# Smaller adaLN weight slabs, the vector part's loads one step ahead, and 512-column runs for the gate's matvec

## The chip, the core and the metric

The kernel runs on one core of one Trainium2 chip. A core has a tensor engine (PE, whose weight loads the profile lists apart as PEld), a vector engine (DVE), a scalar engine (ACT), GpSimd (POOL), the sync engine (SP) that mostly issues DMAs, and 16 DMA engines behind the queues. Each engine works through its own instructions in their order and waits on semaphores for the others. The metric is the device time of one execution in microseconds; less is better.

## The reference

One layer of a flow-matching backbone, for 128 context tokens and 256 latent tokens, D = 2048 channels, all in fp32. What matters here is the modulation that comes from the condition vectors c and c_ctx through the matrix ada_w (2048 x 12288), and where its six parts are used:

```python
def _adaln(cond, ada_w, ada_b):
    mod = jax.nn.silu(cond) @ ada_w + ada_b
    return mod.reshape(cond.shape[0], N_MOD, D_MODEL)
...
shift_a, scale_a, gate_a, shift_f, scale_f, gate_f = [mod[:, i][:, None, :] for i in range(N_MOD)]
h = _rmsnorm(x, norm_w[0]) * (1 + scale_a) + shift_a
proj = h @ w_in
...
q, k, v, o, g, u = jnp.split(proj, [M, 2 * M, 3 * M, 4 * M, 4 * M + N_GATES * N_HEADS], axis=-1)
...
hm, C, n, m = _mlstm_bidir(q, k, v, gates, C0.astype(f32), n0.astype(f32), m0.astype(f32))
...
hp = _pool_mixer(u, pool_w, pool_scale, grid_w)
mix = jnp.concatenate([hm, hp], axis=-1) @ w_out
x = x + gate_a * _rmsnorm(mix, norm_w[1])
h = _rmsnorm(x, norm_w[2]) * (1 + scale_f) + shift_f
y = jnp.square(jax.nn.relu(h @ w1)) @ w2
x = x + gate_f * _rmsnorm(y, norm_w[3])
```

The mLSTM has 8 heads of 128 channels and runs over three chunks of 128 tokens (the context one and two latent ones) in both directions. Each of the six parts i = 0 to 5 of the modulation is a product of two vectors (c_ctx and c) with 2048 columns of ada_w: 16 MB are read for it once.

## The kernel before

**Products.** Every fp32 weight tile of 512 KB is loaded into one of three raw buffers (`load_w`, L114 to L132), split by ACT into a high part (L126) and by DVE into a low part (L127), four buffers of each, and multiplied in three matmuls, L135 to L137 (high by high, low by high, high by low). A tile of q, k or o is 24 such matmuls of 384 columns. The program goes through u and v of the input projection (s = 0 to 7, two channel tiles each), then q and k for four pairs of heads, then o, the output projection wo, and the MLP.

**The modulation.** Shift_a and scale_a (i = 0, 1) are made by the tensor engine ahead of and beside u and v (`first_ada`), 256 columns at a time. `ada_mat` (L203) takes up to four parts of up to 256 columns. A part is 16 rows of ada_w per partition; per 512 KB slab (four rows of 256 columns) it has four matmuls, each with 32 rows of output in its own quarter of the array (rows 32 g to 32 g + 31 of one PSUM bank, g = j mod 4). When all parts have been added up, ACT copies the sum to SBUF (L223), small matmuls on it (L226) turn it into columns, and DVE adds the bias (`ada_finish`, L234). For gate_a (i = 2), `mid_mat` calls it twice with four parts of 256 columns: 34 steps, 32 of them a slab and a group of four matmuls. Scale_f and shift_f (i = 4, 3) are made by DVE: `ada_vec` (L244 to L274) does 512 columns in eight steps, each a load of 512 KB (two rows of 512 columns, L250) and four DVE instructions that multiply and add (L255, L257) into `ada_acc`; then four matmuls add up the partitions (L265), ACT copies (L267), and two small matmuls (L270) make columns: 10 steps for each of eight calls. Gate_f (i = 5) is made in the MLP, by one ada_mat run and three ada_vec runs.

**What sets the order.** `Feed` (L142) gives a side job a number of steps per call, and each product calls its feeds after every weight tile: gate_a 0.75 steps, the vector part 80/76 steps, one step of the attention of the pair of heads before, and so on. In the attention of a pair (names `..._0` to `..._3`), `num` and `cu` are products with v, `C1` is the state that DVE carries to the next chunk (L579), `hs` is the output that DVE normalises (L598, L601), and `hT` (L640) are its transposes on PE. The tile scheduler then lays the instructions of PE, DVE and ACT into one fixed order each. All weight and slab loads go through SP's one queue in one order, where a load waits until its buffer is free, and everything behind it on SP waits too. A load on SP also waits until the eighth load before it has landed.

**Buffers.** The ada slabs share four buffers of 4 KB per partition (tag `ada`, `N_ADA = 4`); in their places the last rows of the gate, `gf` (L923), lie at the end of the MLP. The copies of L223 and L267 share two small tiles (tag `adasb`).

## Time and profile before

| | |
|---|---|
| median of three runs | 1767.98 us (1766.83 to 1768.8) |
| span of the profiled execution | 1766.4 us |
| its instructions | 24738 |
| loads of ada_w | 192 of 512 KB |
| DMA traffic | 326.15 MB, 185 GB/s over the span |

Times in the profile count from the start of the span. A row of the timeline has the start of an instruction or of a run of alike ones, its duration, engine, line, operation, `output<-inputs`, shape and count; brackets at its end tell how long the engine sat idle before it and who released it. A row of the waits has engine and line, what it waited for, the sum in us, the number of times and the longest. A row of the windows has, for each engine, busy time and number of instructions in a stretch of time, then the granted PE clock as a share of full speed, the busy share of the DMA engines and GB/s.

### The profile page before, as it was taken

To read this page: it belongs to the slowest core of one execution; us is meant where nothing else is said; L and a number is where in the kernel's file an instruction comes from. 1 tells how busy PE (TensorE), PEld (TensorE's weight loads), DVE (VectorE), ACT (ScalarE), POOL (GpSimd) and SP (SyncE) were. 2 spreads that over 40 slices of the span, in tenths; PEclk is the share of its full clock that TensorE was granted. 3 is DMA by queue.
4 is the path that set the end of the run, shared out by engine and by line. 5 is a ranking of instruction groups with operands and counts; after the bars stand their busy time and mean duration, and the time that the engine had idled before them with its cause. 6 is when DMAs were issued, how large, how long until landed. Compare 5 with 4: busy or idle time off the path is not lost.

```text
span 1766.4 us, 24738 instructions
## 1 busy us (share of the span) xinstructions
PE 1719.2 (97%) x9643; PEld 1539.2 (87%) x9643; DVE 1067.4 (60%) x1756; ACT 627.3 (36%) x1047; POOL 129.7 (7%) x172
## 2 busy tenths in 40 slices
PE   6999999998999999999999999999999999999997
PEld 3777898887999989988988988988988998998986
DVE  3667877787898849763546644475444443443446
ACT  4322343443434336532432432332332332332332
POOL 0000021222101133110000000000000000000100
PEclk9999999999999999999999999999999999999999
DMA  9888988887777774574345544454434354344543
GB/s 304 279 263 286 299 261 231 253 251 213 232 238 235 237 250 156 185 225 131 120 130 162 175 130 121 130 167 122 129 120 131 120 168 131 120 130 136 165 141 107
DMA packets 250436, 326.15 MB, mean 185 GB/s; under 512 B 14096, under 2 KB 185808, under 8 KB 249936
## 3 DMA queue, kind: packets, MB, share of 16 engines
q1 hardware_dynamic: 242096, 303.74, 54.1%
q0 software_dynamic: 6560, 18.97, 4.3%
q10 hardware_dynamic: 1664, 1.87, 0.3%
q8 instruction: 75, 1.23, 0.3%
q14 instruction: 41, 0.34, 0.1%
HBM read 313.98 MB, written 10.55 MB: 184 GB/s over the span
## 4 chain that ended last, share of the span: by engine, by line
PE 86%; DMA 5%; issue 3%; DVE 2%; POOL 2%; ACT 1%; SPq 0%; ACTq 0%; DVEq 0%; POOLq 0%
PE y L855 10%; PE y L856 10%; PE y L857 10%; PE acc_w L135 9%; PE acc_w L137 9%; PE acc_w L136 9%; DMA ada_raw<-in_ada_w_dram 3%; PE acc_wo L135 3%; PE acc_wo L136 2%; PE acc_wo L137 2%; PE ada L218 2%; PE acc_o L135 1%; PE acc_o L137 1%; PE acc_o L136 1%; PE u L379 1%
## 5 line engine op out<-in xcount | busy, mean ns | idle before, releaser
L127 DVE TENSOR_TENSOR lo_w<-raw_w,hi_w 128x1024 fp32r<-128x1024 f32 x256 | 313.9, 1226 | 440.7 <-ACT hi_w L126 440.3
L126 ACT ACTIVATE hi_w<-raw_w 128x1024 fp32r<-128x1024 f32 x256 | 271.3, 1060 | 666.2 <-PE acc_w L136 302.1
L135 PE MATMUL acc_w<-h2h,hi_w 128*128 128x386 f32 x1024 | 347.8, 341 | 2.4 <-ACT h2h L805 2.4
L137 PE MATMUL acc_w<-h2h,lo_w 128*128 128x386 f32 x1024 | 347.5, 339 | 0.0
L136 PE MATMUL acc_w<-h2l,hi_w 128*128 128x386 f32 x1024 | 347.2, 339 | 0.0
L257 DVE SCALAR_TENSOR_TENSOR ada_acc<-ada_raw,sg,ada_acc 128x512 f32<-128x512 f32 x330 | 237.5, 767 | 21.8 <-DMA ada_raw<-in_ada_w_dram 21.7
L135 PEld LDWEIGHTS acc_w<-h2h,hi_w 128*128 128x128 f32 x1024 | 193.9, 190 | 5.2 <-ACT h2h L805 3.0
L136 PEld LDWEIGHTS acc_w<-h2l,hi_w 128*128 128x128 f32 x1024 | 193.8, 189 | 0.9 <-issue 0.4
L137 PEld LDWEIGHTS acc_w<-h2h,lo_w 128*128 128x128 f32 x1024 | 193.5, 189 | 0.0
L218 PE MATMUL ada<-ada_raw,cT 128*32 128x256 f32 x832 | 61.5, 397 | 5.1 <-DMA ada_raw<-in_ada_w_dram 5.0
L879 DVE TENSOR_TENSOR y<-y,y 128x512 f32<-128x512 f32 x81 | 55.7, 691 | 11.8 <-PE y L857 11.3
L126 ACT ACTIVATE hi_wo<-raw_wo 128x1024 fp32r<-128x1024 f32 x32 | 34.1, 1067 | 67.1 <-PE acc_wo L136 27.9
L846 ACT ACTIVATE z<-z,bz 128x128 f32<-128x128 f32 (+1 forms) x128 | 47.9, 442 | 11.3 <-DVE z L844 11.2
L127 DVE TENSOR_TENSOR lo_wo<-raw_wo,hi_wo 128x1024 fp32r<-128x1024 f32 x32 | 38.7, 1218 | 19.3 <-ACT hi_wo L126 19.3
L379 PE MATMUL v<-hi_v,hh 128*128 128x384 f32 (+1 forms) x144 | 49.0, 341 | 0.0
L381 PE MATMUL v<-hi_v,hl 128*128 128x384 f32 (+1 forms) x144 | 47.2, 328 | 0.0
L380 PE MATMUL v<-lo_v,hh 128*128 128x384 f32 (+1 forms) x144 | 46.9, 326 | 0.0
L774 POOL DMA_DIRECT2D gf_dram<-gfT x1 | 0.5, 519 | 626.8 <-DVE bz L843 626.8
L135 PE MATMUL acc_k<-hh,hi_k 128*128 128x384 f32 x128 | 45.4, 355 | 0.0
L218 PEld LDWEIGHTS ada<-ada_raw,cT 128*32 128x32 f32 x832 | 19.8, 110 | 28.9 <-issue 14.5
L135 PE MATMUL acc_o<-hh,hi_o 128*128 128x384 f32 x128 | 44.7, 349 | 0.0
L135 PE MATMUL acc_q<-hh,hi_q 128*128 128x384 f32 x128 | 44.4, 347 | 0.0
(940 smaller groups left out, 3621.1 us busy)
## 6 DMA issues: line engine op xcount, KB each, us to landing
raw_w<-in_w_dram SPq DMA_DIRECT2D x256, 512.0 KB, 3.7
ada_raw<-in_ada_w_dram SPq DMA_DIRECT2D x192, 512.0 KB, 5.1
raw_wo<-in_w_out_dram SPq DMA_DIRECT2D x32, 512.0 KB, 4.9
raw_u<-in_w_in_dram SPq DMA_DIRECT2D x16, 512.0 KB, 7.4
raw_q<-in_w_in_dram SPq DMA_DIRECT2D x16, 512.0 KB, 5.8
raw_k<-in_w_in_dram SPq DMA_DIRECT2D x16, 512.0 KB, 5.2
raw_o<-in_w_in_dram SPq DMA_DIRECT2D x16, 512.0 KB, 5.3
raw_v<-in_w_in_dram SPq DMA_DIRECT2D x16, 384.0 KB, 7.8
```

Source lines behind the costliest of these rows:

```text
L126: nc.scalar.activation(hi[:, 0:n], raw[:, 0:n], AF.Copy)
L127: low = lambda: nc.vector.tensor_tensor(lo[:, 0:n], raw[:, 0:n], hi[:, 0:n].bitcast(F32), op=ALU.subtract)
L135: nc.tensor.matmul(ps, lh, rh, start=start, stop=False)
L136: nc.tensor.matmul(ps, lh, rl, start=False, stop=False)
L137: mm3.ins = nc.tensor.matmul(ps, ll, rh, start=False, stop=stop).ins
L218: nc.tensor.matmul(ps[32 * g:32 * g + 32, 0:w], cT[:, j, 6 - 2 * b:38 - 2 * b], raw[:, a, :], start=b == 0 and j < 4, stop=b == n - 1 and ...
L257: nc.vector.scalar_tensor_tensor(acc[:, g, :], raw[:, a, :], cj, acc[:, g, :], op0=ALU.mult, op1=ALU.add)
L379: nc.tensor.matmul(acc[i][:, 0:n], xh[:, sl], hi[:, k, :], start=k == 0, stop=False)
L855: nc.tensor.matmul(acc, xh[:, s], hi, start=k == 8 * ch, stop=False)
L856: nc.tensor.matmul(acc, xh[:, s], lo, start=False, stop=False)
L857: nc.tensor.matmul(acc, xl[:, s], hi, start=False, stop=k == 8 * ch + 7)
L879: nc.vector.tensor_tensor(dst, acc[i], dst, op=ALU.add)
```

## The change

- **Slabs.** The ada buffers are eight of 2 KB per partition in place of four of 4 KB: the same 16 KB. A load is 256 KB in place of 512 KB everywhere, so there are twice as many (one part of the very first step, which uses another tag, is left as it was).
- **The gate's run.** `mid_mat` calls ada_mat once with four parts of 512 columns: 17 steps. A step has four loads of 256 KB, one for each of its four matmuls of 512 columns, and there are 16 groups of four in place of 32 groups of four with 256 columns. The sum fills a whole PSUM bank, so the small matmuls behind it go to a second bank. The rate is 17/46 of a step per call.
- **The vector part.** `ada_vec` issues the two loads of a step one step ahead of the DVE work on them, in an 11th step per call. The rate goes from 80/76 to 88/76, so that it takes as many calls as before.
- **Around it.** The copies share one tile of 512 columns in place of two of 256. The tail's gate rows are eight tiles of 512 columns in place of four of 1024. Comments and docstrings are taken out; line numbers shift by up to 15.

```diff
-N_ADA = 4
+N_ADA = 8
...
+    def ada_tile(tag, nj, w, name):
+        return wp.tile([P, nj, w], F32, tag=tag, name=name, bufs=N_W if tag == "lo" else N_ADA)
...
     def ada_mat(parts, tags=("ada",)):
         n, nk = len(parts), parts[0][2]
-        w, nj = nk * P, 8 // nk
+        w = nk * P
         ps = bank(f"ada_{parts[0][0]}_{parts[0][1]}")
         for b, (i, k0, _) in enumerate(parts):
             c0 = i * D + k0 * P
+            tag = tags[b % len(tags)]
+            nj = (8 if tag == "lo" else 4) // nk
             for j0 in range(0, 16, nj):
-                tag = tags[b % len(tags)]
-                raw = wp.tile([P, nj, w], F32, tag=tag, name=f"ada_raw_{i}_{k0}_{j0}", bufs=N_W if tag == "lo" else N_ADA)
+                raw = ada_tile(tag, nj, w, f"ada_raw_{i}_{k0}_{j0}")
                 nc.sync.dma_start(raw, aw[:, j0:j0 + nj, c0:c0 + w])
...
-                if b < n - 1 or j0 + nj < 16:
+                if (j0 + nj) % 4 == 0 and (b < n - 1 or j0 + nj < 16):
                     yield
-        sb = wp.tile([P, 256], F32, tag="adasb", name=f"ada_sb_{parts[0][0]}_{parts[0][1]}", bufs=2)
+        sb = wp.tile([P, 512], F32, tag="adasb", name=f"ada_sb_{parts[0][0]}_{parts[0][1]}", bufs=1)
         nc.scalar.activation(sb[:, 0:w], ps[:, 0:w], AF.Copy)
         yield
+        if w > 256:
+            ps = bank(f"adaf_{parts[0][0]}_{parts[0][1]}")
+        o = 0 if w > 256 else 256
...
     def ada_vec(i, q):
...
+        def load(t):
+            raws = [ada_tile("ada", 1, 512, f"ada_raw_{i}_{q}_{j}")[:, 0, :] for j in (2 * t, 2 * t + 1)]
+            for a, raw in enumerate(raws):
+                nc.sync.dma_start(raw, aw[:, 2 * t + a, c0:c0 + 512])
+            return raws
+
+        raws = load(0)
+        yield
         for t in range(8):
-            raw = wp.tile([P, 2, 512], F32, tag="ada", name=f"ada_raw_{i}_{q}_{t}", bufs=N_ADA)
-            nc.sync.dma_start(raw, aw[:, 2 * t:2 * t + 2, c0:c0 + 512])
+            ahead = load(t + 1) if t < 7 else None
...
+            raws = ahead
...
     def mid_mat():
-        for i, hb in MID[:6 - N_VEC]:
-            yield from ada_mat([(i, 8 * hb + 2 * b, 2) for b in range(4)])
+        yield from ada_mat([(2, 4 * b, 4) for b in range(4)])
...
-    ada1 = Feed(mid_mat(), max(0.75, 17 * (6 - N_VEC) / 76))
-    ada2 = Feed(mid_vec(), 20 * N_VEC / 76)
+    ada1 = Feed(mid_mat(), 17 / 46)
+    ada2 = Feed(mid_vec(), 88 / 76)
...
-            for hf in range(2):
-                t = wp.tile([P, 1024], F32, tag="ada", name=f"gf{g}{hf}", bufs=N_ADA)
+            for q in range(4):
+                t = ada_tile("ada", 1, 512, f"gf{g}{q}")[:, 0, :]
```

The scheduler lays the instructions out anew. Three places follow, each before and then changed. The first is SP's queue at the end of the last k tiles, where o begins; `ada_raw_4_3_t` are the slabs of the fourth vector run of scale_f, `ada_raw_2_...` those of gate_a.

```order
L120 DMA raw_k_1792_3_4199<-in_w_in_dram 128x4x256
L250 DMA ada_raw_4_3_0_4151<-in_ada_w_dram 128x2x512
L120 DMA raw_o_3072_0_4259<-in_w_in_dram 128x4x256
L214 DMA ada_raw_2_10_4_4187<-in_ada_w_dram 128x4x256
L120 DMA raw_o_3072_1_4307<-in_w_in_dram 128x4x256
L120 DMA raw_o_3072_2_4383<-in_w_in_dram 128x4x256
L250 DMA ada_raw_4_3_1_4193<-in_ada_w_dram 128x2x512
L214 DMA ada_raw_2_10_8_4241<-in_ada_w_dram 128x4x256
L250 DMA ada_raw_4_3_2_4247<-in_ada_w_dram 128x2x512
L120 DMA raw_o_3072_3_4438<-in_w_in_dram 128x4x256
```

```order
L118 DMA raw_o_3072_2_4552<-in_w_in_dram 128x4x256
L258 DMA ada_raw_4_3_0_4312<-in_ada_w_dram 128x512
L258 DMA ada_raw_4_3_1_4313<-in_ada_w_dram 128x512
L258 DMA ada_raw_4_3_2_4346<-in_ada_w_dram 128x512
L258 DMA ada_raw_4_3_3_4347<-in_ada_w_dram 128x512
L258 DMA ada_raw_4_3_4_4396<-in_ada_w_dram 128x512
L258 DMA ada_raw_4_3_5_4397<-in_ada_w_dram 128x512
L258 DMA ada_raw_4_3_6_4404<-in_ada_w_dram 128x512
L258 DMA ada_raw_4_3_7_4405<-in_ada_w_dram 128x512
L216 DMA ada_raw_2_8_12_4460<-in_ada_w_dram 128x512
L216 DMA ada_raw_2_8_13_4463<-in_ada_w_dram 128x512
L118 DMA raw_o_3072_3_4603<-in_w_in_dram 128x4x256
```

Before, three vector slabs of 512 KB are spread over this stretch and the fourth stands behind raw_o_3072_3; changed, the same 2 MB of the run (eight halves) stand ahead of raw_o_3072_3 in one piece.

The second place is DVE while k of the second pair of heads is multiplied and the attention of the first pair (`..._0_...`) runs beside it. `lo_k_1280_n` are the low parts of the four k tiles, `C1_0_2_1` the state that the products `num_0_1` on PE need.

```order
L553 TENSOR_TENSOR mbc_0_2719<-sk2_0_2844,mbc_0_2719 128x2x256
L257 SCALAR_TENSOR_TENSOR ada_acc_4_1_2863<-ada_raw_4_1_1_2960,sg_107,ada_acc_4_1_2863 128x512
L257 SCALAR_TENSOR_TENSOR ada_acc_4_1_2863<-ada_raw_4_1_2_3030,sg_107,ada_acc_4_1_2863 128x512 x4
L127 TENSOR_TENSOR lo_k_1280_2_3109<-raw_k_1280_2_3106,hi_k_1280_2_3108 128x1024
L257 SCALAR_TENSOR_TENSOR ada_acc_4_1_2863<-ada_raw_4_1_3_3100,sg_107,ada_acc_4_1_2863 128x512
L623 COPY nout_2073<-C1_0_0_0_2900 128x2
L623 COPY nout_2073<-C1_0_0_1_2907 128x2
L579 SCALAR_TENSOR_TENSOR C1_0_1_0_2914<-C0_0_0_2725,gbc_0_2720,cu_0_1_0_2915 128x129 x2
```

```order
L271 SCALAR_TENSOR_TENSOR ada_acc_4_1_2999<-ada_raw_4_1_5_3161,sg_107,ada_acc_4_1_2999 128x512 x2
L125 TENSOR_TENSOR lo_k_1280_1_3179<-raw_k_1280_1_3176,hi_k_1280_1_3178 128x1024
L271 SCALAR_TENSOR_TENSOR ada_acc_4_1_2999<-ada_raw_4_1_6_3168,sg_107,ada_acc_4_1_2999 128x512 x2
L271 SCALAR_TENSOR_TENSOR ada_acc_4_1_2999<-ada_raw_4_1_7_3169,sg_107,ada_acc_4_1_2999 128x512
L638 COPY nout_2193<-C1_0_0_0_3034 128x2
L638 COPY nout_2193<-C1_0_0_1_3041 128x2
L594 SCALAR_TENSOR_TENSOR C1_0_1_0_3048<-C0_0_0_2849,gbc_0_2844,cu_0_1_0_3049 128x129 x2
L271 SCALAR_TENSOR_TENSOR ada_acc_4_1_2999<-ada_raw_4_1_7_3169,sg_107,ada_acc_4_1_2999 128x512
L610 TENSOR_TENSOR dn_0_0_0_3068<-dn_0_0_0_3068,ecol_2191 128x2
L610 TENSOR_TENSOR dn_0_0_1_3078<-dn_0_0_1_3078,ecol_2191 128x2
L125 TENSOR_TENSOR lo_k_1280_2_3257<-raw_k_1280_2_3254,hi_k_1280_2_3256 128x1024
L594 SCALAR_TENSOR_TENSOR C1_0_2_1_3054<-C0_0_1_2852,gbc_0_2844,cu_0_2_1_3055 128x129 x2
```

Before, the low parts 0 and 1 of k_1280 stood ahead of everything shown here, with one vector slab (four instructions) ahead of them; changed, lo_k_1280_1 stands behind twelve of the vector instructions (slabs 4_1_0 to 4_1_5), and lo_k_1280_2 behind sixteen, between the two state updates.

The third place is PE at the last tile of q of the third pair. L218 and L220 are the same line of ada_mat, L265 and L280 the matmuls that add up a vector run's partitions, and L285 (before L270) the small ones behind ACT's copy.

```order
L218 MATMUL ada_2_0_2261<-ada_raw_2_6_4_3375,cT_105 32x256 x4
L265 MATMUL adav_4_1_3381<-ada_acc_4_1_2863,cst_69 32x256 x4
L135 MATMUL acc_q_512_0_3206<-hh12_1631,hi_q_512_3_3390 128x384
L136 MATMUL acc_q_512_0_3206<-hl12_1632,hi_q_512_3_3390 128x384
L137 MATMUL acc_q_512_0_3206<-hh12_1631,lo_q_512_3_3391 128x384
L135 MATMUL acc_q_512_1_3207<-hh12_1631,hi_q_512_3_3390 128x384
```

```order
L220 MATMUL ada_2_0_2465<-ada_raw_2_4_8_3521,cT_105 32x512
L220 MATMUL ada_2_0_2465<-ada_raw_2_4_9_3524,cT_105 32x512
L220 MATMUL ada_2_0_2465<-ada_raw_2_4_10_3527,cT_105 32x512
L220 MATMUL ada_2_0_2465<-ada_raw_2_4_11_3530,cT_105 32x512
L280 MATMUL adav_4_1_3533<-ada_acc_4_1_2999,cst_69 32x256 x4
L133 MATMUL acc_q_512_0_3346<-hh12_1735,hi_q_512_3_3548 128x384
L134 MATMUL acc_q_512_0_3346<-hl12_1736,hi_q_512_3_3548 128x384
L135 MATMUL acc_q_512_0_3346<-hh12_1735,lo_q_512_3_3549 128x384
L285 MATMUL adav_4_1_3533<-cst_69,adav_sb_4_1_3538 128x4 x2
L133 MATMUL acc_q_512_1_3347<-hh12_1735,hi_q_512_3_3548 128x384
```

A group of four waits for four tiles now, each with its own load, and the small matmuls of this vector run, which stood 32 rows behind L265, follow it after three; the same holds for three more of the eight vector runs of i = 4 and 3.

26 lines of the change are left out of this document (12 added, 14 removed).

## The prediction

> **What bounds the kernel now.** First the page's busy times and its chain of work, then the windows, one for each stage.
>
> ```profile
> PE 1719.2 (97%) x9643; PEld 1539.2 (87%) x9643; DVE 1067.4 (60%) x1756; ACT 627.3 (36%) x1047; POOL 129.7 (7%) x172
> PE 86%; DMA 5%; issue 3%; DVE 2%; POOL 2%; ACT 1%; SPq 0%; ACTq 0%; DVEq 0%; POOLq 0%
> 30.00:186.00 156.00, 150.78 (x1059) 116.92 (x1057) 103.21 (x212) 53.01 (x88) 0.83 (x2) 0.99 0.86 279
> 270.00:440.00 170.00, 155.30 (x1036) 142.47 (x1035) 129.67 (x277) 67.98 (x183) 36.31 (x45) 0.97 0.82 240
> 440.00:650.00 210.00, 210.00 (x1292) 201.70 (x1292) 171.28 (x267) 79.44 (x148) 31.37 (x38) 1.00 0.74 235
> 715.00:1766.00 1051.00, 1041.94 (x5220) 936.89 (x5218) 540.43 (x744) 347.45 (x478) 27.29 (x42) 1.00 0.45 141
> ```
>
> PE is the bound: idle 47 of 1766 us. So a change pays through PE's own work, or through the 14.7 us that PE stands still in 270 to 440, where q, k and attention share it, or the 5.2 us in u and v. The MLP, 1051 us, keeps the order of its work. The waits of PE, in 270 to 330, 330 to 440 and 30 to 186 in turn:
>
> ```profile
> PE adav L270 <- ACT adav_sb L267: 3.1, 1, 3.1
> PE hT L640 <- DVE hs L601: 1.6, 1, 1.6
> ```
> ```profile
> PE hT L640 <- DVE hs L601: 8.0, 1, 8.0
> PE ada L226 <- ACT ada_sb L223: 2.0, 1, 2.0
> ```
> ```profile
> PE ada L218 <- DMA ada_raw<-in_ada_w_dram: 3.9, 5, 1.8
> ```
>
> All five are waits for modulation work or for DVE work queued behind it. The largest, followed on the timelines of DVE, PE and SP:
>
> ```profile
> 419.52 0.16 DVE L187 TENSOR_SCALAR rsh<-ssh 128x2 f32<-128x2 f32 x1
> 427.02 0.75 DVE L257 SCALAR_TENSOR_TENSOR ada_acc<-ada_raw,sg,ada_acc 128x512 f32<-128x512 f32 x1 [7.33 <-DMA ada_raw<-in_ada_w_dram]
> 427.69 0.42 DVE L601 TENSOR_TENSOR hs<-hs,rsh 128x256 f32<-128x256 f32 x1
> 428.16 1.12 PE L640 MATMUL hT<-cst,hs 128*128 128x128 f32 x4 [7.95 <-DVE hs L601]
> 397.09 0.37 SPq L250 DMA_DIRECT2D ada_raw<-in_ada_w_dram  x1
> 406.53 0.37 SPq L214 DMA_DIRECT2D ada_raw<-in_ada_w_dram  x1
> 409.25 0.37 SPq L250 DMA_DIRECT2D ada_raw<-in_ada_w_dram  x1
> 415.85 0.37 SPq L250 DMA_DIRECT2D ada_raw<-in_ada_w_dram  x1
> 428.00:432.00 4.00, 3.84 (x19) 2.70 (x20) 4.00 (x9) 1.33 (x5) 0.00 (x0) 0.58 0.32 101
> ```
>
> One vector instruction stands ahead of the last hs on DVE, and its slab (the fourth of run 4_3) was issued only at 415.85: SP stood from 397 to 406 because the four slab buffers were in use. After the stall the granted clock is 0.58 for 4 us, which costs about 4 x 0.42 = 1.7 us more.
>
> **The change part by part.**
>
> *The gate's groups.* A lone group of four matmuls of 256 columns between two 384-column ones, and three groups in a row:
>
> ```profile
> 486.87 0.34 PE L136 MATMUL acc_o<-hl,hi_o 128*128 128x384 f32 x1
> 487.04 0.34 PE L137 MATMUL acc_o<-hh,lo_o 128*128 128x384 f32 x1
> 487.31 0.64 PE L218 MATMUL ada<-ada_raw,cT 128*32 128x256 f32 x8
> 487.88 0.44 PE L135 MATMUL acc_o<-hh,hi_o 128*128 128x384 f32 x1
> 488.16 0.34 PE L136 MATMUL acc_o<-hl,hi_o 128*128 128x384 f32 x1
> 36.69 1.50 PE L218 MATMUL ada<-ada_raw,cT 128*32 128x256 f32 x24
> 38.12 0.50 PE L379 MATMUL u<-hi_u,hh 128*128 128x512 f32 x1
> 506.31 0.51 PE L226 MATMUL ada<-cst,ada_sb 128*128 128x8 f32 x4
> 506.68 0.42 PE L135 MATMUL acc_o<-hh,hi_o 128*128 128x384 f32 x1
> ```
>
> The big matmuls follow each other at some 0.175 (486.87 to 487.04). From 487.04 to 488.16 is 1.12; less two steps of 0.175 the lone group costs 0.77. In the row of three, a group costs (38.12 - 36.69)/3 = 0.48, so 256 columns stream in at most 0.48 and some 0.3 is the price of breaking in. A group of 512 columns then costs 0.77 + 0.45 = 1.2. 32 x 0.77 - 16 x 1.2 = **-5.4 us**; with 1.4 a group it would be -2.2, with 1.05 -7.8. One small finish goes too (506.31 to 506.68 and its break-in, some 0.5), and with it the 2.0 wait for the first run's copy: **-2.5** (-0.5 if the one copy left waits as long).
>
> *The vector part, 4_3.* Changed, slabs 4_3_0 to 4_3_7 (the same data as the four late loads) go out in a row behind raw_o_3072_2. The ring of eight lets 4_3_0 to 4_3_3 go early; 4_3_4 to 4_3_7 need the buffers of gate_a's 2_8_8 to 2_8_11, and that group on PE now stands right behind the second chunk's products. Here and for the next item I walk along the rows:
>
> ```profile
> 409.69 0.39 PE L592 MATMUL num<-C,gbc 128*128 128x129 f32 x2
> raw_v<-in_w_in_dram SPq DMA_DIRECT2D x8, 256.0 KB, 2.9
> ada_raw<-in_ada_w_dram SPq DMA_DIRECT2D x13, 512.0 KB, 5.6
> ```
>
> The products end at 410.1 and the group at 411.3; a load of 256 KB lands in 2.9 when nothing is ahead, so 4_3_7, the fourth, at about 416 (5.6, the median of 270 to 330 for 512 KB, gives 419). DVE then has some 5.5 us of work up to hs_2: 421 to 422, where PE arrives at 420 (two tiles of 24 x 0.175 = 4.2 each). The stall shrinks from 8.0 to about 1.5: **-6.5**, and most of the slow clock goes: **-1.2**. If the slabs land no earlier than now, both are 0.
>
> *The vector part, 4_1.*
>
> ```profile
> 280.25 1.05 ACT L126 ACTIVATE hi_q<-raw_q 128x1024 fp32r<-128x1024 f32 x1
> 281.20 1.05 ACT L126 ACTIVATE hi_k<-raw_k 128x1024 fp32r<-128x1024 f32 x1
> 282.14 0.38 ACT L267 ACTIVATE adav_sb<-adav 128x256 f32<-128x256 f32 x1
> 282.57 0.61 PE L270 MATMUL adav<-cst,adav_sb 128*128 128x4 f32 x4 [3.13 <-ACT adav_sb L267]
> 292.95 1.95 PE L574 MATMUL cu<-v,wk 128*128 128x129 f32 x16
> 298.81 0.59 DVE L579 SCALAR_TENSOR_TENSOR C<-C,gbc,cu 128x129 f32<-128x129 f32 x2
> 300.61 0.38 PE L589 MATMUL num<-v,mbc 128*128 128x129 f32 x2
> 320.29 0.66 PE L640 MATMUL hT<-cst,hs 128*128 128x128 f32 x4 [1.60 <-DVE hs L601]
> ```
>
> On ACT the copy of 4_0 now comes ahead of the two splits that stood before it (280.25 and 281.20), so it is done near 279.4, and PE gets there then (282.57 less its idle 3.1): **-2.9**. But DVE gets 4_1 later: 4_1_0 is loaded behind raw_k_1280_2, and 4_1_4 waits for the group of 2_0_12 to 2_0_15, near 286 on PE (279.4, a finish of 0.6, a tile of 4.2, scores of 0.8, the group's 1.2). From 282 on DVE is nearly full, with twelve vector instructions ahead of lo_k_1280_1 and sixteen ahead of C1_0_2_1. With 0.7 each, C1_0_2_1 is ready near 300.4; before, at 299.4. PE would be at num_0_1, now 300.61, at 297.6 (286.2, a tile, 3.0 for cu and num from 292.95 on, a tile): **+2.8** (0 if DVE catches up, 6 if each load takes 5.6). Behind it the walk has hs_0_2 at 316.5 and PE at hT_0 at 317.8: **-1.6**.
>
> *Small things.* Four of the eight small finishes follow three to five matmuls (0.5 to 0.9) behind L280 instead of 24 or more; ACT's copy takes 0.38 and must be released: +0.5 (0 to 4). A group of four waits for the last of its four loads: +1 (0 to 4). The attentions of the second and last pair have the same coupling as 4_1 and no wait today that could go: +2 (0 to 6). In u and v, from the fourth period on, raw_u goes ahead of the second part's slabs, which land up to 2 us later while 3.9 us of waits for slabs stand there already: +0.5 (-1 to +8). Twice the loads on SP at 0.37 each are covered while SP waits for buffers, as from 397 to 406; without that cover 188 more are 70 us. Loading a step ahead by itself costs and brings nothing: SP already runs ahead as far as its buffers go, and these hold the same 2 MB. The eight tiles of the tail are loaded long before the end, on POOL, which is 7% busy; uncovered they would cost a load or two, 5 us.
>
> By the Trainium skill (DMA: Bandwidth & Descriptors, Bandwidth) transfers should be batched to 1 MiB or more to reach three quarters of the peak, which speaks against halving these. Its fit in Anatomy of one DMA, 2.0 us fixed plus bytes over 436 GB/s, gives an estimate of 2.6 us for 256 KB and 3.2 for 512 KB, where the trace has 2.9 for the first. If the fixed parts came one after another, the 62 loads that u and v have more (64 now, two of them left as they are) would cost 124 us by it. The trace does not bear that out: loads overlap, and u and v move 279 GB/s with loads of about 512 KB.
>
> The sum: -5.4 - 2.5 - 6.5 - 1.2 - 2.9 + 2.8 - 1.6 + 0.5 + 1 + 2 + 0.5 = **-13.3 on a span of 1766.4**. Waits that are removed early are partly paid again at the next stage's loads (DMA share 0.82 in this window); I take 3 back for that, so -10: span 1756, and with the 1.6 us by which the median lies above the span, **1758**.
>
> **Rivals.**
>
> *The ring couples PE and DVE (slower).* A gate step takes four of eight buffers; the vector run's next loads start only when PE has passed that group, and PE soon waits for DVE behind these slabs. For it: 4_1_4 and 4_3_4 above, and 11.2 us from the issue at 415.85 to the use at 427.02. Against: the median 5.6. If a load takes 11 us in place of 3.5, DVE is 7.5 late in the two attentions walked above, 6.3 of it on PE (C1 has a slack of 1.2 from 299.40 to 300.61), and 1 or so in the other two: +15 on top of today's waits, less PE's own 7.9: +7, **1775**. It decides from a landing of about 7 us on.
>
> *Only PE's own work shrinks.* The waits move but do not go, as the first copy and hT would meet DVE anyway: -5.4 - 0.5 + 1: **1763**. For it: DVE is busy 130 of 170 us. Against: each wait has a named late slab or copy.
>
> *u and v become bound by loads.* DMA share there is 0.86, and raw_u is ahead of slabs that already came late. Eight parts 1.5 us later are +12 on the -10: **1770**. The rule of the Trainium skill on batching would show here too. For it: 3.9 us of waits now. Against: the same bytes in 279 GB/s.
>
> *The load ahead does nothing*, since buffers and not issue set the time: then the vector terms go by the ring alone, which is what I costed.
>
> **How the numbers follow.** A measurement tells 0.2%, 3.5 us, from no change. My forecast 0.46 (own range 1752 to 1764), all faster; only PE's work 0.16 (0.11 faster, 0.05 same); u and v bound 0.14 (0.03 faster, 0.06 same, 0.05 slower); the ring 0.24, slower, with 0.02 of it the same. That is 0.60 faster, 0.13 same, 0.27 slower. The range takes in the second and third rival and most of the ring: 1749 to 1776.
>
> **What would show it.** Groups of 512 columns: the gap around a lone one is near 1.2, and 16 of them. hT L655 has a wait of 3 or less near 415 and no clock of 0.6 behind it. adav L285 near 280 waits under 1. num_0_1 waits for C1 or acc_k for lo_k near 295: 0 to 6. PE busy in u and v stays at 150 or more of 156. It is wrong if PE waits for lo_k or hs in several attentions for 5 us or more each, or if slabs in u and v are waited for by more than 10 us in all.

## The result: slower, by 0.4%

The changed kernel takes 1775.37 us (median of four runs, 1774.87 to 1778.62) against 1767.42 for the kernel before (four runs, 1766.83 to 1768.8): ratio 1.0043, 95% interval 1.0028 to 1.0058. Forecast was 1758 in 1749 to 1776: the range holds the time, but only because the slower rivals had been taken into it; the forecast itself went the wrong way. The span of the profiled execution is 1773.6 us, 7.2 more than before.

The changed kernel: busy time of each engine, the window of u and v, and the mean granted clock; the last row is the clock of the kernel before.

```profile
PE 1721.9 (97%) x9515; PEld 1540.3 (87%) x9515; DVE 1065.5 (60%) x1748; ACT 628.6 (35%) x1046; POOL 133.6 (8%) x176
30.00:186.00 156.00, 151.24 (x1047) 114.88 (x1046) 103.34 (x211) 52.61 (x88) 0.82 (x2) 1.00 0.89 277
core 0: 1773.6 us, clock 0.991
core 0: 1766.4 us, clock 0.994
```

PE is still the bound. It is busy 2.7 us longer with 128 records fewer, because part of its work ran at a lower clock: 1773.6 x 0.009 = 16.0 us of clock lost, where the kernel before (clock 0.994) lost 10.6. The clock is given to 0.001, which is 1.8 us, so this difference is rough. Its idle time grew from 47.2 to 51.7. So idle 4.5 and busy 2.7 make the 7.2. The waits of PE in 270 to 330, 330 to 440 and 440 to 660 (engine and line, what it waited for, sum, times, longest):

```profile
PE num L607 <- DVE C L594: 1.7, 1, 1.7
```
```profile
PE hT L655 <- DVE hs L616: 8.0, 2, 4.7
PE s L554 <- ACT k L533: 4.1, 1, 4.1
```
```profile
PE cu L589 <- DVE wk L580: 4.0, 2, 2.4
```

Of the waits that the prediction wanted gone, the one for adav_sb (3.1 before) and the one for ada_sb (2.0) are gone, and the 8.0 at the third hT is down to 3.3. In their place stand three that the kernel before does not have: 4.7 at the second hT, 4.1 at the scores of the second pair (s), and 4.0 in the last pair (cu). What DVE waited for in 270 to 440 tells where the first two come from. First the kernel before, then the changed one:

```profile
DVE ada_acc L257 <- DMA ada_raw<-in_ada_w_dram: 17.2, 6, 7.3
DVE ws L559 <- DMA mbc<-m_dram: 10.9, 5, 5.5
```
```profile
DVE ws L574 <- DMA mbc<-m_dram: 21.6, 6, 5.6
DVE ada_acc L271 <- DMA ada_raw<-in_ada_w_dram: 3.8, 2, 3.5
```

The change did to the slabs what it should, 17.2 to 3.8. But the wait for another load doubled: `mbc`, the stabilisers of a pair of heads, read from DRAM to all 128 partitions through POOL's queue. No term of the prediction speaks of it. At the second hT and the scores of the second pair it reads as follows; POOL issues mbc behind the power of rsh, DVE meets it at ws, ACT at the exponential of ws:

```profile
310.85 1.61 POOL L186 TENSOR_TENSOR rsh<-rsh,mhalf 128x2 f32<-128x2 f32 x1 [5.12 <-DVE rsh L185]
312.42 0.78 POOL L543 DMA_DIRECT2D mbc<-m_dram  x1
313.91 0.76 POOL L543 DMA_DIRECT2D mbc<-m_dram  x1
325.75 0.30 DVE L574 TENSOR_TENSOR ws<-acol,mbc 128x2 f32<-128x2 f32 x3 [5.64 <-DMA mbc<-m_dram]
326.09 0.21 ACT L575 ACTIVATE ws<-ws 128x8 f32<-128x8 f32 x1 [10.10 <-DVE ws L574]
330.92 0.85 ACT L533 ACTIVATE k<-acc_k 128x384 f32<-128x384 f32 x2
316.91 0.82 PE L655 MATMUL hT<-cst,hs 128*128 128x128 f32 x6
331.45 2.07 PE L554 MATMUL s<-q,k 128*128 128x128 f32 x8 [4.14 <-ACT k L533]
374.07 0.23 DVE L574 TENSOR_TENSOR ws<-acol,mbc 128x2 f32<-128x2 f32 x2 [5.41 <-DMA mbc<-m_dram]
375.22 0.42 DVE L616 TENSOR_TENSOR hs<-hs,rsh 128x256 f32<-128x256 f32 x1 [0.84 <-POOL rsh L186]
375.70 1.11 PE L655 MATMUL hT<-cst,hs 128*128 128x128 f32 x4 [4.73 <-DVE hs L616]
```

PE is at the first hT at 316.91, 3.4 us ahead of the kernel before (320.29). It keeps none of it. POOL issues the second load of mbc at 313.91, where the kernel before does so at 311.67, because rsh comes later from DVE; the load is used 11.8 us after its issue (11.3 before). Then ws, the exponentials and the copy of k follow in order on DVE and ACT, and the scores start at 331.45 (329.94 before). Around 375 the order of DVE makes it worse: ws for the third pair stands *ahead* of the last hs of the second, and PE waits for that hs. The wait in the last pair has another cause. DVE waits for two slabs of the vector part, and wk, which PE needs for cu, stands behind them:

```profile
437.53 2.74 DVE L271 SCALAR_TENSOR_TENSOR ada_acc<-ada_raw,sg,ada_acc 128x512 f32<-128x512 f32 x4 [3.54 <-DMA ada_raw<-in_ada_w_dram]
451.79 1.41 DVE L271 SCALAR_TENSOR_TENSOR ada_acc<-ada_raw,sg,ada_acc 128x512 f32<-128x512 f32 x2 [2.21 <-DMA ada_raw<-in_ada_w_dram]
454.19 1.61 PE L589 MATMUL cu<-v,wk 128*128 128x129 f32 x12 [1.53 <-DVE wk L580]
```

So of the 12.8 us of new waits, 8.8 stand behind mbc and 4.0 behind slabs. After such waits PE runs at half its clock: the matmuls behind the second hT follow each other at 0.32, not at 0.175, and the windows around the stalls at s, the second hT and the third hT show it (the clock is the third number from the end):

```profile
376.93 0.52 PE L134 MATMUL acc_q<-hl,hi_q 128*128 128x384 f32 x1
377.25 0.52 PE L135 MATMUL acc_q<-hh,lo_q 128*128 128x384 f32 x1
```
```profile
330.00:337.00 7.00, 5.55 (x23) 5.55 (x24) 4.32 (x5) 5.03 (x11) 0.00 (x0) 0.55 0.80 237
373.00:381.00 8.00, 5.30 (x19) 5.30 (x20) 2.21 (x9) 0.21 (x1) 0.72 (x1) 0.57 0.88 209
428.00:432.00 4.00, 3.24 (x12) 3.24 (x13) 2.29 (x4) 0.00 (x0) 0.94 (x2) 0.57 0.96 258
```

By the Trainium skill (TensorE: Matmul & The Clock Gate, Part 1: The HAM clock gate) the array falls to half rate after at least one idle window of some 3.4 us, and the window runs freely. The stalls of 4.1 and 4.7 agree, but here shorter waits were enough: 3.3 at the third hT, and in the kernel before the 2.0 for ada_sb, around which the clock was 0.79 in 364 to 372. The length alone does not decide either. In front of the MLP both kernels have one wait of 2.4; before it was followed by full clock, in the changed kernel by half rate:

```profile
661.00:667.00 6.00, 5.25 (x29) 5.25 (x30) 6.00 (x19) 4.33 (x13) 0.00 (x0) 1.00 0.59 191
```
```profile
669.00:675.00 6.00, 5.71 (x24) 5.72 (x24) 6.00 (x18) 4.34 (x13) 0.00 (x0) 0.72 0.60 202
```

That is 6 x 0.28 = 1.7 us of the 5.4, with no new stall in front of it.

### The profile page after: what moved, and what is told of

Read it like the earlier page. It is cut to its first block, busy times and chain, and to the rows that moved or that the text cites. A ratio compares the mean times of both kernels' runs of the same rounds, so it can differ in the third digit from the quotient of the medians.

```text
span 1773.6 us, 24927 instructions
## 1 busy us (share of the span) xinstructions
PE 1721.9 (97%) x9515; PEld 1540.3 (87%) x9515; DVE 1065.5 (60%) x1748; ACT 628.6 (35%) x1046; POOL 133.6 (8%) x176
## 4 chain that ended last, share of the span: by engine, by line
PE 86%; DMA 6%; issue 3%; DVE 3%; POOL 1%; ACT 1%; SPq 0%; ACTq 0%; DVEq 0%; POOLq 0%
PE y L869 10%; PE y L870 10%; PE y L871 10%; PE acc_w L134 10%; PE acc_w L133 10%; PE acc_w L135 10%; DMA ada_raw<-in_ada_w_dram 3%; PE acc_wo L133 2%; PE acc_wo L135 2%; PE acc_wo L134 2%; PE ada L220 2%; PE v L394 1%; PE acc_o L133 1%; PE acc_o L134 1%; PE acc_o L135 1%
## 5 line engine op out<-in xcount | busy, mean ns | idle before, releaser
L220 PE MATMUL ada<-ada_raw,cT 128*32 128x256 f32 (+1 forms) x704 | 64.8, 435 | 4.8 <-DMA ada_raw<-in_ada_w_dram 4.1
L893 DVE TENSOR_TENSOR y<-y,y 128x512 f32<-128x512 f32 x81 | 55.9, 691 | 12.2 <-PE y L871 11.8
L220 PEld LDWEIGHTS ada<-ada_raw,cT 128*32 128x32 f32 x704 | 19.2, 109 | 30.8 <-DMA ada_raw<-in_ada_w_dram 14.7
L135 PE MATMUL acc_q<-hh,lo_q 128*128 128x384 f32 x128 | 44.3, 346 | 0.0
```

The source lines that it names most:

```text
L135: mm3.ins = nc.tensor.matmul(ps, ll, rh, start=False, stop=stop).ins
L220: nc.tensor.matmul(ps[32 * g:32 * g + 32, 0:w], cT[:, j, 6 - 2 * b:38 - 2 * b], raw[:, a, :], start=b == 0 and j < 4, stop=b == n - 1 and ...
L893: nc.vector.tensor_tensor(dst, acc[i], dst, op=ALU.add)
```

## The experiments

Each ratio is to the kernel before, measured beside it on the same chip (its medians there were 1769.8 to 1771.8), with its 95% interval. "wo" is how much later (+) or earlier than in the kernel before PE starts the output projection, 516.30 there, in the one profiled execution. Times of one kernel scatter by some 0.3% from run to run, so the ratio decides and the profile only tells where. The expectations that are in microseconds were written against the 1767.4 of the first comparison; the ratios times 1767.4 can be held against them.

| kernel | edit | ratio | interval | wo |
|---|---|---|---|---|
| (the change) | | 1.0043 | 1.0028 to 1.0058 | +7.5 |
| e1_gate_only | half slabs, wide groups, no load ahead | 1.0026 | 1.0014 to 1.0039 | +9.8 |
| e2_ahead_only | half slabs, load ahead, old groups | 1.0016 | 1.0004 to 1.0029 | +7.0 |
| e3_slabs_only | half slabs alone | 1.0041 | 1.0023 to 1.0058 | +7.5 |
| e6_old_slabs | wide groups alone | 1.0015 | 1.0003 to 1.0027 | +7.4 |
| e4_mbc_early | change, mbc early | 0.998 | 0.9959 to 1.0001 | -4.3 |
| e5_before_mbc | before, mbc early | 0.9974 | 0.9954 to 0.9993 | -6.3 |
| e7_old_slabs_mbc | e6, mbc early | 0.997 | 0.9954 to 0.9985 | -6.0 |
| e8_ring10 | change, 10 half slabs | 0.998 | 0.9965 to 0.9995 | -2.5 |
| e9_slot53 | change, 53 slots | 1.0028 | 1.0015 to 1.0041 | +5.2 |
| e10_before_ring5 | before, 5 whole slabs | 0.9965 | 0.9952 to 0.9979 | -7.8 |
| e11_mbc_ring9 | change, mbc early, 9 half slabs | 1.0031 | 1.0019 to 1.0043 | -0.2 |
| e12_mbc_ring10 | change, mbc early, 10 half slabs | 0.9928 | 0.9914 to 0.9942 | -17.4 |
| e13_ws_behind | change, ws behind hs | 1.0023 | 1.0014 to 1.0032 | +6.4 |
| e14_before_ws_behind | before, ws behind hs | 0.9996 | 0.9986 to 1.0006 | +4.6 |
| e15_ring10_ws_behind | e8, ws behind hs | 0.9975 | 0.9962 to 0.9988 | -4.1 |
| e16_before_ring5_ws | e10, ws behind hs | 0.9929 | 0.9915 to 0.9944 | -9.6 |
| e17_before_mbc_ring5 | before, mbc early, 5 whole slabs | 0.9948 | 0.9928 to 0.9968 | -10.9 |
| e18_gate_mbc_ring5 | e7, 5 whole slabs | 0.9966 | 0.9955 to 0.9978 | -7.3 |

### Which part of the change costs

e1 takes the load ahead out of the changed kernel:

```diff
-        raws = load(0)
-        yield
         for t in range(8):
-            ahead = load(t + 1) if t < 7 else None
+            raws = load(t)
...
-    ada2 = Feed(mid_vec(), 88 / 76)
+    ada2 = Feed(mid_vec(), 80 / 76)
```

> The changed kernel, but the vector part loads each step's two slabs at the step that uses them (10 steps, 80/76 a call, as before); half-size slabs and the gate's run of 512 columns stay. Before 1767.4, changed 1775.4. If loading ahead is what makes the vector slabs and then DVE late (it keeps four of the eight buffers for one vector run while a gate step takes the other four), this gives the gate's saving without the loss: 1762 to 1766, with u and v still about 2 later than before. If the gate's step of 1 MB is the cause, it stays at 1773 or more.

e2 takes the wide groups out; e3 takes out both, so that only the halved slabs are left:

```diff
-        yield from ada_mat([(2, 4 * b, 4) for b in range(4)])
+        for hb in range(2):
+            yield from ada_mat([(2, 8 * hb + 2 * b, 2) for b in range(4)])
...
-    ada1 = Feed(mid_mat(), 17 / 46)
+    ada1 = Feed(mid_mat(), 0.75)
```

> Half-size slabs and the vector part one step ahead, but the gate in two runs of 256 columns as before. If loading ahead is the cause: 1775 to 1782 (the loss without the gate's saving of 5 to 6). If the gate's step of four slabs is: 1767 to 1771, the load ahead costing nothing.

> Only the slabs are changed (eight of 256 KB for four of 512 KB); gate and vector part as before. If the half-size loads and their place behind raw_u cost u and v their 2.1 us and nothing else: 1768.5 to 1770.5. If halving them is harmless (the new order in u and v being by chance): 1766.5 to 1768.5. If more loads on SP's queue make the mid stage late: 1773 or more.

e6 leaves the slabs as they were (four of 4 KB, loaded at their use) and widens only the gate's groups, with two slabs for each:

```diff
-                if b < n - 1 or j0 + nj < 16:
+                if (j0 + nj) % 4 == 0 and (b < n - 1 or j0 + nj < 16):
...
-        for i, hb in MID[:6 - N_VEC]:
-            yield from ada_mat([(i, 8 * hb + 2 * b, 2) for b in range(4)])
+        yield from ada_mat([(2, 4 * b, 4) for b in range(4)])
...
-    ada1 = Feed(mid_mat(), max(0.75, 17 * (6 - N_VEC) / 76))
+    ada1 = Feed(mid_mat(), 17 / 46)
```

> Of the change only the gate's groups of 512 columns, with the slabs left as they were (four buffers of 4 KB, two slabs for each group, vector part loading at its use). Theory C (PE's own saving is real and the halved slabs with their new order cost it): ratio 0.995 to 0.998, so about 1759 to 1764, the waits in 270 to 440 within 3 us of the 14.7 before. Rival D (any move of the gate's groups brings new waits of PE and half-speed spells behind them, whatever the slabs): ratio 1.001 to 1.005. Rival E (groups of 512 need two slabs at once, so PE waits at them): slab waits of PE over 5 us beyond those before.

Taken so, e1 is at 1772.0, e2 at 1770.2 and e3 at 1774.6. e1 rules out that the load ahead costs it all, and e1 (just short of 1773) and e2 together speak for the gate's step of four slabs; but e3, which has no such step, costs as much as the whole change. So no single part is the culprit: halved slabs alone cost as much as all of it, the wide groups alone cost too (e6 is in rival D's range), and all four intervals lie above 1. In e1 and e3 stalls stand at the same places, but there a slab is behind them. In e1 the second hT waits 10.8, in e3 the first 6.1; the instruction of DVE that stood ahead of the last hs, with its wait:

```profile
378.49 0.75 DVE L269 SCALAR_TENSOR_TENSOR ada_acc<-ada_raw,sg,ada_acc 128x512 f32<-128x512 f32 x1 [7.64 <-DMA ada_raw<-in_ada_w_dram]
```
```profile
324.07 0.75 DVE L269 SCALAR_TENSOR_TENSOR ada_acc<-ada_raw,sg,ada_acc 128x512 f32<-128x512 f32 x1 [3.82 <-DMA ada_raw<-in_ada_w_dram]
```

### The loads of mbc, a pair earlier

e4 gives mbc two buffers, and issues the loads of the next pair in the first step of a pair, so that they have a whole attention in which to land. Three slots are given up for the room.

```diff
-N_SLOT = 56
+N_SLOT = 53
...
+    def load_mbc(hp):
+        mbc = att.tile([P, 2, 3, 2, P], F32, tag="mbc", name=f"mbc_{hp}", bufs=2)
+        for d in range(2):
+            nc.gpsimd.dma_start(mbc[:, d], m_dram[d, :, 2 * hp:2 * hp + 2, :].partition_broadcast(P))
+        return mbc
...
-        mbc = att.tile([P, 2, 3, 2, P], F32, tag="mbc", name=f"mbc_{hp}", bufs=1)
+        mbc = mbcs.pop(hp) if hp in mbcs else load_mbc(hp)
...
+        if hp < 3:
+            mbcs[hp + 1] = load_mbc(hp + 1)
         yield
```

> The changed kernel with the broadcast load mbc of the next pair of heads issued one attention earlier into a second buffer (three of 56 slots given up for the room). If the new stalls at s_1 (4.1) and hT_1 (4.7) come from mbc, which POOL issues only behind the rsh of the attention before, they and the slow clock behind them go: 1762 to 1767, wherever the slabs land. If PE waits there for the vector slabs ahead of the same DVE work, the waits move to other tiles: 1773 or more.

e5 makes the same edit in the kernel before, e7 in e6.

> The kernel before, with the mbc loads of the next pair of heads issued one attention early (as in e4_mbc_early) and nothing else. Theory A (the change made DVE wait for mbc, where the kernel before did not, so e4 only undid a loss of the change): ratio to before 0.998 to 1.002, no stall of PE shorter by more than 1 us. Rival B (the early mbc loads are a gain of their own, of the 8 us that e4 had over the changed kernel): ratio 0.994 to 0.997.

> e6_old_slabs with the early mbc loads. Theory C with A: like e6 within 0.2%. With B: 0.990 to 0.994, better than both e5 and e6. Rival D: over 1.

Early loads gain in the kernel before as well: e5 is 0.26% faster than it. That lies between the ranges of theory A and rival B, with an interval that reaches into both; A falls by its other sign, since waits of PE did shrink (adav_sb from 3.1 to 0.4, the third hT from 8.0 to 2.6). From the change to e4 the ratio goes from 1.0043 to 0.998 (0.63%, give or take 0.26), and that is 0.37 more than in the kernel before, give or take 0.32: just clear of noise. From e6 to e7 it is 0.45% (0.20), which is not clear of the 0.26. e7 is as fast as e5, above what B gave for it: with early mbc the wide groups bring nothing on top. In e4 s went from 4.1 to 1.6 as expected, hT did not: 5.7 are left at the second, for with its data loaded early, the scheduler moved ws of the *last* pair up in front of that hs, where it waits for the next load.

```profile
373.95 0.23 DVE L583 TENSOR_TENSOR ws<-acol,mbc 128x2 f32<-128x2 f32 x2 [4.85 <-DMA mbc<-m_dram]
```

### The slab ring

e8 is the changed kernel with `N_ADA = 10`, e10 the kernel before with `N_ADA = 5` (the same 20 KB), both with 53 slots; e9 is the changed kernel with 53 slots and nothing else, since e4, e5, e7 and e8 share that number.

> The changed kernel with ten 2 KB buffers in place of eight (three slots given up for them). Ring theory (eight buffers couple PE and DVE): the slab waits of DVE ahead of hs and of the last attention (5.4, 3.5 and 2.2 us in the changed kernel) shrink by half or more, 1766 to 1770. Theory A (the POOL queue's mbc loads and the in-order DVE behind them): within 0.15% of the changed kernel, 1773 to 1778.

> The changed kernel with 53 slots in place of 56, the only thing that e4, e5, e7 and e8 share beside their own edits. If the slots explain part of their gains: ratio to before 0.998 to 1.001. If they do nothing, it stays at the changed kernel's 1.0043: 1.003 to 1.006, with u and v ending 0.7 to 2.5 us after the kernel before, as in all kernels with eight half slabs.

> The kernel before with five 4 KB slab buffers in place of four (53 slots), the same bytes as the ten halves of e8_ring10. If the time in e8 comes from a deeper ring alone: 0.994 to 0.998, u and v 2 to 4 us shorter. If four whole slabs never bound the kernel before and only eight halves did (so that e8 undid a loss of the change): 0.999 to 1.002.

The slots do little: 1.0028, just under what no effect was to give, with an interval that overlaps the changed kernel's. The ring does more: 0.63% from the change to e8 (0.21 either way), 0.35% in the kernel before. But e8's expectation was wrong on the place. Its 5.4 was a wait for mbc and no slab; DVE's slab waits in 270 to 440 did not halve but rose from 3.8 to 10.3, and PE waits longer at hT than in the changed kernel. The waits at s and in the last pair are gone.

```profile
PE hT L655 <- DVE hs L616: 15.9, 2, 9.5
```

The gain is in the last pair, in u and v, and in groups that wait for their slabs without PE being shown idle (PEld is the weight load in front of the matmul). PEld's waits at these groups over the whole execution, in the kernel before, the changed kernel and e8, and the window of u and v in e8:

```profile
PEld ada L218 <- DMA ada_raw<-in_ada_w_dram: 7.3, 9, 2.3
```
```profile
PEld ada L220 <- DMA ada_raw<-in_ada_w_dram: 14.7, 24, 2.0
```
```profile
PEld ada L220 <- DMA ada_raw<-in_ada_w_dram: 3.5, 9, 0.6
```
```profile
30.00:186.00 156.00, 153.93 (x1097) 120.32 (x1096) 107.75 (x222) 54.89 (x93) 0.00 (x0) 1.00 0.91 292
```

292 GB/s against 277 in the changed kernel: u and v end 4.3 us earlier than before in e8 and 5.9 in e10, and 0.7 to 3.0 later in the seven kernels with eight half slabs (the change, e1 to e4, e9, e13). But the kernels with four whole slabs scatter too, from 2.8 earlier (e7) to 1.3 later (e14) than the kernel before. So a ring of 16 KB bounds u and v; that it does so more in halves is not clear of this scatter.

e11 and e12 put both together: e4 with nine half slabs (52 slots) and with ten (50 slots).

> e4_mbc_early with nine half slabs (52 slots). If mbc and the ring are two separate causes of the loss, their gains add: half of what e8_ring10 brought on top of e4, 0.994 to 0.996. If they are one wait seen from two sides: 0.997 to 0.999, as either alone.

> e4_mbc_early with ten half slabs (50 slots). Two separate causes: 0.990 to 0.994, the fastest of all. One cause: 0.997 to 0.999. If 50 slots are too few, new waits for slots in u and v: over 1.

e12 is what two separate causes would give: 0.9928, 0.52% below e4 and e8 each. DVE's waits for mbc in 270 to 440 are down to 4.8, PE's at hT to 2.1, and the clock is 0.995:

```profile
DVE ws L583 <- DMA mbc<-m_dram: 4.8, 2, 3.9
```

e11, one buffer less, is a miss for both expectations: 1.0031. In its order ws of the last pair stands ahead of the second pair's last hs, as in e4; there PE waits 7.5, and it starts the output projection 17 us later than e12. In e12's order it stands behind. The rest is lost later: from there to the end e11 takes 1261.2, e12 1256.0, and the kernel before 1250.1. Behind it are waits of PE in the MLP that neither the kernel before nor the change has, and half clock after them:

```profile
PE x1t L852 <- ACT x1tok L854: 4.5, 2, 4.1
```

Another 2.8 come at y for the same x1tok, which ACT holds back until POOL's stores of earlier ones to DRAM are done. All twelve kernels with fewer than 56 slots have this wait (0.7 in e8, 1.0 in e9, 4.1 in e4, 4.5 in e12), and none of the eight with 56. So part of what early mbc and the ring gain is probably paid back here for the slots given up; why it is 0.7 in one kernel and 7.3 in another stays open.

### The order of ws and hs

The place of ws in DVE's order is the scheduler's choice, and it differs from kernel to kernel. Rows of the order around the second pair's last hs, in the kernel before, the change and e12:

```
464 L601 TENSOR_TENSOR hs_1_2_3591<-hs_1_2_3591,rsh_2075 128x256
474 L559 TENSOR_TENSOR ws_2_3818<-acol_2070,mbc_2_3770 128x2 x4

472 L574 TENSOR_TENSOR ws_2_3971<-acol_2190,mbc_2_3909 128x2 x2
474 L616 TENSOR_TENSOR hs_1_2_3737<-hs_1_2_3737,rsh_2195 128x256
476 L574 TENSOR_TENSOR ws_2_3971<-acol_2190,mbc_2_3909 128x2 x2

478 L625 TENSOR_TENSOR hs_1_2_3740<-hs_1_2_3740,rsh_2195 128x256
486 L583 TENSOR_TENSOR ws_3_4510<-acol_2190,mbc_3_3921 128x2 x4
```

One rule puts ws behind the last hs of the pair before; in e13 it moves the two instructions of row 472 behind row 474, and nothing else on any engine.

```diff
-            nc.vector.tensor_tensor(hs, hs, rsh[:, i, h0:h0 + 2].unsqueeze(2).to_broadcast([P, 2, P]), op=ALU.mult)
+            outputs.ins = nc.vector.tensor_tensor(hs, hs, rsh[:, i, h0:h0 + 2].unsqueeze(2).to_broadcast([P, 2, P]), op=ALU.mult).ins
...
+        with ExitStack() as es:
+            if last_hs:
+                es.enter_context(tc.issue_after(last_hs[-1]))
...
+        last_hs.append(outputs.ins)
```

> The changed kernel with one rule for the scheduler: the ws of the next pair (DVE instructions that read the broadcast load mbc) stand behind the last hs of the pair before. Only ws_2 moves, by one place, from ahead of hs_1_2 to behind it. Order theory (DVE stands in its fixed order at ws for a load that is not there, and PE pays at hT): hT_1's wait falls from 4.7 to 1 or less, the half-speed spell behind it goes or shrinks, 3 to 6 us of the loss come back, ratio 1.000 to 1.002. Latency theory (mbc's landing itself is late for the next scores, whatever the order): the wait moves to s_2 or k behind it, ratio 1.003 to 1.005 as the changed kernel.

> The kernel before with the same rule. There two ws stand ahead of hs_0_2 and of hs_2_2 but none ahead of hs_1_2. Order theory: hT_0's 1.6 goes; hT_2's 8.0 stays, since a slab and not ws is behind it: 0.998 to 1.000. If the kernel before owed its time to a lucky order, nothing is gained: 0.999 to 1.002.

> e8_ring10 with the same rule. There two ws stand ahead of hs_0_2, hs_1_2 and hs_2_2, and PE waits 2.2, 6.4 and 9.5 at hT. Order theory: these fall to 4 or less in all, 10 to 16 us come back with the half-speed spells: 0.989 to 0.993. Latency theory: 0.996 to 0.999, the waits move to k and s.

> e10_before_ring5 with the same rule, so the kernel before with both causes taken away: its 8.1 at hT_0 (four ws ahead of hs_0_2) falls to 2 or less: 0.991 to 0.994. Against e15_ring10_ws_behind it tells what the change itself is worth when neither the ring nor the order of ws takes it back: by the prediction's own terms e15 is 5 to 10 us below e16; if the change brings nothing of its own they are equal within 3 us.

In e13 the waits of PE in 330 to 440 become:

```profile
PE s L556 <- ACT k L533: 7.6, 2, 4.7
PE ada L220 <- DMA ada_raw<-in_ada_w_dram: 1.7, 1, 1.7
PE hT L661 <- DVE hs L621: 0.8, 1, 0.8
```

hT went from 8.0 to 0.8 and s from 4.1 to 7.6: the stall has two layers. Take the order away, and the next scores still wait for the load, by ACT, which stands at ws for 10 us and has the copy of k behind it. The ratio (1.0023) lies between what the two theories expected, and its interval overlaps the changed kernel's. e14 gained nothing, as both allowed. e16 answered to the order theory in its time (0.36% below e10) and nearly in its wait (hT from 8.1 to 3.1, where 2 or less was asked). e15 answered to the latency theory: it is where e8 is, inside that theory's range; the second hT went from 6.4 to 0.4, and 5.1 at s came in its place. The third hT still waits 9.9, and there the ring is at work, on SP and DVE:

```profile
402.65 6.67 SPq L216 DMA_DIRECT2D ada_raw<-in_ada_w_dram  x4
410.61 7.55 SPq L258 DMA_DIRECT2D ada_raw<-in_ada_w_dram  x6
422.83 0.75 DVE L271 SCALAR_TENSOR_TENSOR ada_acc<-ada_raw,sg,ada_acc 128x512 f32<-128x512 f32 x1 [7.94 <-DMA ada_raw<-in_ada_w_dram]
```

SP takes 14 us for the gate's four slabs and six of the vector part behind them, though an issue alone takes 0.37; one vector instruction ahead of the last hs waits 7.9 for its slab, and PE 9.9 behind it.

### What the change is worth without both

e17 is the kernel before with early mbc and five whole slabs (50 slots), to be set against e12; e18 is e7 with five whole slabs (50 slots).

> The kernel before with early mbc loads and five whole slabs (50 slots): e12_mbc_ring10 (0.9928) without the change. If the gate's wide groups save their 5 us on PE once loads no longer take it back: 0.994 to 0.997, 3 us or more above e12. If the change is worth nothing even there: 0.991 to 0.994. Its waits: no ws stands ahead of the last hs of the second and third attention, so under 3 at each hT.

> e7_old_slabs_mbc (the gate's wide groups, whole slabs, early mbc) with five slabs (50 slots). In its instruction order two ws, of the last pair, stand ahead of hs_1_2; they read a load that was issued only shortly before. Order theory: PE waits 4 to 8 at the second hT, as in e4 and e11, and nothing else is large: 0.992 to 0.996; without that wait it would be at e12's 0.993 or below. Latency theory (an early load can't hurt): no wait over 2 at hT, 0.989 to 0.992.

e12 over e17 is 0.998, give or take 0.0024: with both causes gone the change may be worth up to some 8 us or nothing, which these runs do not tell apart. With one cause gone it is worth nothing that shows: e4 over e5 is 1.0006 (0.0029 either way), e8 over e10 1.0015 (0.0020). The loss of 0.43% thus shrinks when mbc, the ring or both are out of the way, which is the best evidence that they carry it. Against it stands e15 over e16, 1.0046 (0.0019): with a deep ring and ws behind hs the change still costs as much as before. e17 itself lies where the wide groups were to save their 5 us, but its first hT waits 3.3, and the pair leaves that saving unproven. e18 came out just above the order theory's range, and PE waits 8.4 at the second hT, some more than it gave; but ws is only 1.1 of it; a slab that also stands ahead of the last hs is the rest:

```profile
369.30 0.75 DVE L260 SCALAR_TENSOR_TENSOR ada_acc<-ada_raw,sg,ada_acc 128x512 f32<-128x512 f32 x1 [5.48 <-DMA ada_raw<-in_ada_w_dram]
```

So it is not ws as such: whatever reads a late load and stands ahead of the last hs sets PE's arrival.

## Why the prediction was wrong

**The gate's groups (-5.4): the price was right.** A lone group of 512 columns between two 384-column matmuls:

```profile
489.88 0.34 PE L135 MATMUL acc_o<-hh,lo_o 128*128 128x384 f32 x1
490.15 1.06 PE L220 MATMUL ada<-ada_raw,cT 128*32 128x512 f32 x8
491.14 0.44 PE L133 MATMUL acc_o<-hh,hi_o 128*128 128x384 f32 x1
491.43 0.34 PE L134 MATMUL acc_o<-hl,hi_o 128*128 128x384 f32 x1
```

From 489.88 to 491.43 is 1.55; less two steps of 0.175 it is 1.2, as forecast. The finish and its wait for ada_sb (-2.5) went too. That this work shortened the end is not shown in any run: e6, which has it alone, is slower than the kernel before, and e7 is no faster than e5.

**The vector part, 4_1: right, up to the first hT.** adav_sb's copy starts at 279.23 and PE reaches L285 without a wait:

```profile
279.23 0.37 ACT L282 ACTIVATE adav_sb<-adav 128x256 f32<-128x256 f32 x1
280.02 0.51 PE L285 MATMUL adav<-cst,adav_sb 128*128 128x4 f32 x4
297.60 0.38 PE L604 MATMUL num<-v,mbc 128*128 128x129 f32 x2
```

PE is at num at 297.60, where the walk had it, C1 costs 1.7 where 2.8 was forecast, and the first hT is at 316.9 without a wait (the walk: 317.8).

**The vector part, 4_3 (-6.5): the slab came, the size was off.** The wait at the third hT is 3.3, not 1.5, and the slow clock of 1.2 that was to go is still there: 0.57 in 428 to 432, where the kernel before had 0.58.

**The step that failed** is the one among the small things: the other attentions "have the same coupling as 4_1 and no wait today that could go: +2 (0 to 6)". There was a wait that could come: s 4.1 and hT 4.7 in the second pair and 4.0 in the last, that is 12.8, 10.8 more than taken and twice the upper bound. For the 8.8 in the second pair the reason is that the walks ended at hT. They followed PE, DVE and SP, and not POOL's queue, on which mbc for the next pair is issued only when DVE has delivered rsh; behind it stand ws on DVE and ACT and the copy of k. The profile of before had the rows: DVE's 10.9 for mbc, ACT's 6.6 at 323.25, and a median landing of 8.5. The 4.0 in the last pair are the coupling itself, DVE behind late slabs, at a place that was not walked.

Two more terms were mis-sized. The clock was to win 1.2 and lost 5.4, 6.6 off, of which 1.7 fell in front of the MLP. And the 3 us taken back for "waits that are removed early" and paid again later were meant for just such a thing and far too few. The third hT adds 1.8, u and v 1.6 (2.1 measured, 0.5 forecast, inside its bounds and inside the scatter between kernels).

Waits, clock, third hT and u and v make 20.8, and from the -13.3 of the sum to the +7.2 measured it is 20.5. That is a rough balance and its closeness is in part luck: half clock inside a wait is counted twice, C1 came out 1.1 better than forecast, and the -5.4 of the groups is taken as gained though no run shows it.

```profile
311.67 0.77 POOL L528 DMA_DIRECT2D mbc<-m_dram  x1
323.25 0.21 ACT L560 ACTIVATE ws<-ws 128x8 f32<-128x8 f32 x1 [6.62 <-DVE ws L559]
mbc<-m_dram POOLq DMA_DIRECT2D x8, 384.0 KB, 8.5
```

By the Trainium skill's fit (DMA: Bandwidth & Descriptors, Anatomy of one DMA — SWDGE (gpsimd) path) a load of 384 KB from POOL's queue would be an estimate of 2.9 us. The trace does not agree, with 8.5 before and 9.1 after: such a load belongs in a walk at its measured landing. That section of the Trainium skill is on loads from POOL; the slabs, to which the prediction put the same fit, go through SP's queue.

**The rivals.** The time is the slower rival's, 1775, and its mechanism is there in part: the 4.0 in the last pair stand behind slabs, PEld's waits for slabs doubled (7.3 to 14.7), a deeper ring brings 0.63% back, and in e15 SP shows it. But it was put at the two attentions that the prediction walked, with loads of 11 us; the changed kernel's slabs of 256 KB landed in 4.4 at the median, below the 7 from which it was to decide, and the larger part of the new waits is mbc's. That its time came out is luck. "u and v bound by loads" has the right sign and is 6 times too large (2.1 of 12), and PE's own waits for slabs there fell from 3.9 to 2.7. "Only PE's own work" is out by its time. "The load ahead does nothing" is wrong for DVE, whose slab waits in 270 to 440 it takes down by 13 us (e1 16.9, the change 3.8) or 6 (e3 15.5, e2 9.5); no run shows a gain in time from it (e1 1.0026, the change 1.0043).

**Against its own list.** The lone group: right. hT, now at 428.76: 3.3 where 3 or less was asked, and a clock of 0.57 behind it: wrong. adav near 280: right. num: right. u and v at 150 busy or more: 151.2, right. Slabs in u and v waited for by more than 10 us: PE itself 2.7, its weight loads 10.8, so not as PE's waits. "Wrong if PE waits for hs in several attentions for 5 us or more": it waited 4.7 and 3.3, and 4.1 for k, below that bound and enough together.

What stays open: why ten half slabs with early mbc gain so much more than nine, how much the slots given up cost in the MLP, why the change still costs 0.46% with the deep ring and the order rule, and how much of each kernel's time is the scheduler's order alone, since every edit here reshuffled it.

## What to carry to other kernels

Before a wait is counted as gain, walk on to the next thing that the freed engine needs, through *every* queue that feeds it, and give each load its measured landing; a broadcast load behind compute on POOL's queue is easily missed because PE does not wait for it while PE itself is late (DVE did, 10.9 us in the kernel before). Where a scheduler lays an engine's work into one order, read from that order what stands ahead of the instruction on which the bound engine waits: any reader of a load there is a wait as long as the load is late. And where several edits cure a loss, run them in the kernel before as well as in the changed one: early mbc and a deeper ring took 0.63% each off the changed kernel and 1.15% together, nearly the sum, so they are separate causes; but they gain 0.26% and 0.35% without the change too, so not all of that was its loss.
